# A hybrid decoder layer: the down-projection as seven half-size block products in a phase of its own

## The chip, the cores and the metric

One core of one Trainium2 chip. The metric is the device time of one execution in microseconds (us), as the median of several runs. The kernel is written in Python and fully unrolled. TensorE (PE) multiplies, VectorE (DVE), ScalarE (ACT) and GpSimd (POOL) do elementwise work, and SyncE (SP) issues the DMA transfers. At its end the text is scheduled for a simulated timeline (line 984, `schedule_with_timeline_sim=True`): the order of instructions on each engine comes from there, not from the text.

## The reference

S = 2048 tokens, D = 1024 channels, DFF = 4096, float32:

```
x = x + mix @ w_out                        # mix: gated sum of two attention branches
h2 = rmsnorm(x, ln2_g)
x = x + square(relu(h2 @ w_up)) @ w_down   # w_up: 1024 x 4096, w_down: 4096 x 1024
```

All that stands before (the first norm, the combined input projection, both attentions and the gates) is not touched by the change.

## The kernel before, in words

**Precision.** Each operand of a product is split into a high and a low part of the type float32r: ACT casts the source to the high part (line 91), and DVE or POOL subtracts it from the source for the low part (line 92). `mm3` (lines 94 to 98) makes a product from three matmuls: high x high, low x high, high x low. A matmul takes 128 x 128 stationary and 128 x 512 moving elements, and is preceded by its weight load (PEld).

**Out-projection** (lines 772 to 801). For each of 16 blocks of 128 tokens, `load_mix` loads the mixed activations and x, and splits the former. 2 x 8 x 3 matmuls go to two PSUM banks, DVE adds them to x (line 795), and x is stored to `x2_dram` (line 796). `norm2_pre` forms the RMS scale and the scaled block `hn` (lines 753 to 757). `norm2_post`, one block later, transposes it on PE (line 765), scales it by the norm's gain (line 768) and stores it to `h2_dram` in two transfers of 256 KB whose runs are 512 bytes (line 770).

**MLP** (lines 814 to 966). It goes over two halves of 1024 tokens. The up-projection of a half is made in 16 chunks of 256 columns (f), each a 2 x 2 block matrix product by seven products of half-size blocks instead of eight. A11, A12, A21 and A22 are blocks of w_up, B11 to B22 blocks of the token half (B: which half of D, which 512 tokens). S1 to S4 are sums of the A's and T1 to T4 of the B's. `token_operands` (lines 829 to 856) loads a half from `h2_dram` in four slabs, forms T1 to T4 and splits the seven operands, at the start of each half. `up_operands` (lines 858 to 889) does so for the weights of one chunk, with the sums (line 869) and the low parts on POOL. `up_products` (lines 901 to 939) issues the seven products, 7 x 12 matmuls, into four banks, and combines, squares (lines 913 and 927) and splits the results into `us`, which stay on chip. `down_operands` (lines 891 to 899) loads and splits 2 x 128 rows of w_down, in each half anew. Then 8 blocks x 2 column halves x 2 x 3 = 96 matmuls (line 961) form the chunk's part of the down-projection, and DVE adds each bank to x2 (line 962). At the last chunk the sums are stored to `out` (line 964).

**Buffers.** Most loads pass three shared buffers of 4 KB a partition (`raw`, line 81). PSUM has eight banks (`bank`, line 84). SP's queue issues all the transfers.

Of the kernel before, what the change touches and what calls it, by code (L numbers as in the profile page):

```python
# [20 lines left out]
F32 = mybir.dt.float32  # L21
F32R = mybir.dt.float32r
# [3 lines left out]
ALU = mybir.AluOpType  # L26
# [33 lines left out]
def hybrid_layer(tc, x, positions, ln1_g, w_in, q_norm_a, k_norm_a, q_norm_b, k_norm_b, sinks,  # L60
# [687 lines left out]
    x2_dram = dram.tile([S, D], F32, name="x2_dram")  # L748
    h2_dram = dram.tile([P, KD, S], F32, name="h2_dram")
    x2, hn = {}, {}  # L750
    mpool = pools["A"]

    def norm2_pre(i):
        xt = x2[i]
        rs = rms_scale(xt, tmp(f"junky{i}", BF16, (P, D)), mpool, i, "y")
        hn[i] = B4(f"hn{i}", F32)
        nc.vector.tensor_scalar(hn[i], xt, rs, None, op0=ALU.mult)

    def norm2_post(i):
        xt = hn.pop(i)  # L760
        for half in range(2):
            pt = bank(f"h2ps{i}_{half}")
            for j in range(4):
                k = 4 * half + j
                nc.tensor.transpose(pt[:, j * P:(j + 1) * P], xt[:, k * P:(k + 1) * P], ident)
            ks = slice(4 * half, 4 * half + 4)
            t2 = tmp(f"h2t_{i}_{half}").rearrange("p (j t) -> p j t", j=4)
            nc.vector.tensor_tensor(t2, pt.rearrange("p (j t) -> p j t", j=4),
                                    g2T[:, ks].unsqueeze(2).broadcast_to([P, 4, P]), op=ALU.mult)
            nc.sync.dma_start(h2_dram[:, ks, i * P:(i + 1) * P], t2)  # L770

    def load_mix(i):
        r = raw(f"rmix{i}")
        nc.sync.dma_start(r.rearrange("p (k t) -> p k t", k=KD), mix_dram[:, :, i * P:(i + 1) * P])
        mx = B4(f"mh{i}"), B4(f"ml{i}")
        split(mx[0], mx[1], r)
        x2[i] = B4(f"x2_{i}", F32)
        nc.sync.dma_start(x2[i], x[i * P:(i + 1) * P, :])
        return mx

    wo = []
# [4 lines left out]
    mx = load_mix(0)  # L786
    for i in range(NB):
        nxt = load_mix(i + 1) if i + 1 < NB else None
# [8 lines left out]
        if i > 0:  # L797
            norm2_post(i - 1)
        norm2_pre(i)
        mx = nxt  # L800
    norm2_post(NB - 1)
    for pool in (pools["B"], pools["A"], pools["w"]):
        pool.release()
# [7 lines left out]

    MF = FC // P
    NF = DFF // FC
    SP = [tc.alloc_tile_pool(name="mS", bufs=1, reuse_waits="tile"),
          tc.alloc_tile_pool(name="mD", bufs=1, reuse_waits="tile"),
          tc.alloc_tile_pool(name="mF", bufs=1, reuse_waits="tile"),
          tc.alloc_tile_pool(name="mT", bufs=1, side=RIGHT, reuse_waits="tile"),
          tc.alloc_tile_pool(name="mX", bufs=1, side=RIGHT, reuse_waits="tile")]  # L820
    poolS, poolD, poolF, poolT, poolX = SP
    up_src = w_up.rearrange("(h k p) n -> h p k n", p=P, h=2)
    B_NAMES = ("B11", "T1", "T2", "B21", "T3", "T4", "B22")
    A_NAMES = ("A11", "S1", "S2", "A12", "S3", "A22", "S4")

    def Ft(name):
        return poolF.tile([P, 512], F32, tag="f", bufs=5, name=name)

    def token_operands(hf):

        ops = {n: [poolT.tile([P, 4, 512], F32R, tag="t", bufs=14, name=f"{n}{e}{hf}") for e in "hl"]
               for n in B_NAMES}
        ts = slice(1024 * hf, 1024 * hf + 1024)
        for k in range(4):
            r1, r2 = raw(f"rh1_{hf}_{k}"), raw(f"rh2_{hf}_{k}")
            nc.sync.dma_start(r1, h2_dram[:, k, ts])
            nc.sync.dma_start(r2, h2_dram[:, k + 4, ts])
            b11, b12, b21, b22 = r1[:, 0:512], r1[:, 512:1024], r2[:, 0:512], r2[:, 512:1024]

            def put(n, src, eng):  # L840
                split(ops[n][0][:, k, :], ops[n][1][:, k, :], src, eng)

            put("B11", b11, nc.vector)
            t1, t2 = Ft(f"t1_{hf}_{k}"), Ft(f"t2_{hf}_{k}")
            nc.gpsimd.tensor_tensor(t1, b12, b11, op=ALU.subtract)
            put("T1", t1, nc.vector)
            nc.vector.tensor_tensor(t2, b22, t1, op=ALU.subtract)
            put("T2", t2, nc.vector)
            put("B21", b21, nc.gpsimd)
# [138 lines left out]
```

## Time and profile before

| | |
|---|---|
| median of 3 runs | 2913.75 us (2912.76 to 2917.43) |
| the profiled execution | 2914.77 us; its span, first to last instruction, 2912.7 us |
| busy share of the span | PE 97%, weight loads 81%, DVE 55%, POOL 45%, ACT 37% |
| mean granted PE clock | 0.983 of full |
| DMA traffic | 227 MB, 78 GB/s |

The profile is of one execution. Busy is the time in which an engine ran instructions; the weight loads overlap the matmuls, and matmuls overlap one another in the records, so the pace of PE is read from the number of them in a stretch. The granted clock is the share of PE's 2.4 GHz that the chip let it have.

### The profile page before, as it was taken

What the parts mean: (1) busy time and instruction counts of PE and PEld (TensorE: products, weight loads), DVE (VectorE), ACT (ScalarE), POOL (GpSimd) and SP (SyncE); (2) the same over time, 40 slices, a digit from 0 to 9 for tenths busy, and PEclk for the clock granted to TensorE, in tenths of its full rate; (3) what the DMA queues carried; (4) which work ended last, traced back from release to release, by engine and by line L of the source; (5) the groups of instructions that cost most, each with busy time, mean ns of one, the idle gap of its engine ahead of it and who ended that gap; (6) DMA issues with size and microseconds to landing.
All of it is one profiled execution on the core that took longest, in us unless ns stands there. A gap on an engine that the chain in (4) does not pass through costs nothing.

```text
span 2912.7 us, 37930 instructions
## 1 busy us (share of the span) xinstructions
PE 2827.6 (97%) x14281; PEld 2358.1 (81%) x14281; DVE 1598.6 (55%) x2987; ACT 1069.4 (37%) x2203; POOL 1314.8 (45%) x1148
## 2 busy tenths in 40 slices
PE   7999999999989999999996999999998999999999
PEld 6888888887867888888884888888886788888887
DVE  8777675669984114112336555455557654555455
ACT  5566565667884113112113222222223322222221
POOL 5556666676652111111006545544455654445542
PEclk9999999999999999999996999999999999999999
DMA  5321010011145125224554111111115211111111
GB/s 165 93 73 50 12 55 12 14 56 45 56 123 160 58 66 172 67 67 131 180 174 170 60 46 58 52 57 39 56 58 182 79 59 51 46 49 59 51 58 65
DMA packets 210152, 227.42 MB, mean 78 GB/s; under 512 B 13344, under 2 KB 174128, under 8 KB 209968
## 3 DMA queue, kind: packets, MB, share of 16 engines
q1 hardware_dynamic: 209968, 225.00, 24.6%
q8 instruction: 112, 1.84, 0.3%
q14 instruction: 72, 0.59, 0.1%
HBM read 170.23 MB, written 54.72 MB: 77 GB/s over the span
## 4 chain that ended last, share of the span: by engine, by line
PE 90%; DVE 5%; DMA 2%; POOL 1%; issue 1%; ACT 1%; SPq 0%; POOLq 0%; DVEq 0%; ACTq 0%
PE pd L96 9%; PE pd L97 9%; PE pd L98 9%; PE pg L96 4%; PE pg L98 4%; PE pg L97 4%; PE psA L96 4%; PE psA L97 3%; PE psA L98 3%; PE pb L96 3%; PE pb L97 3%; PE pb L98 3%; PE sp L416 2%; PE pt L461 2%; PE po L97 2%; PE po L96 2%
## 5 line engine op out<-in xcount | busy, mean ns | idle before, releaser
L962 DVE TENSOR_TENSOR x2m<-x2m,pd 128x512 f32<-128x512 f32 x512 | 328.6, 682 | 135.7 <-PE pd L98 135.7
L96 PE MATMUL pd<-wdh,uh 128*128 128x512 f32 x1024 | 398.7, 389 | 0.9 <-ACT uh L91 0.7
L97 PE MATMUL pd<-wdl,uh 128*128 128x512 f32 x1024 | 398.4, 389 | 0.0
L92 POOL TENSOR_TENSOR wdl<-rwd,wdh 128x1024 fp32r<-128x1024 f32 x64 | 152.4, 2405 | 468.1 <-ACT wdh L91 468.1
L98 PE MATMUL pd<-wdh,ul 128*128 128x512 f32 x1024 | 362.1, 389 | 0.5 <-DVE ul L92 0.5
L96 PEld LDWEIGHTS pd<-wdh,uh 128*128 128x128 f32 x1024 | 192.2, 188 | 42.0 <-ACT uh L91 1.7
L98 PEld LDWEIGHTS pd<-wdh,ul 128*128 128x128 f32 x1024 | 192.2, 188 | 40.8 <-DVE ul L92 0.9
L97 PEld LDWEIGHTS pd<-wdl,uh 128*128 128x128 f32 x1024 | 192.2, 188 | 39.9
L91 ACT CAST wdh<-rwd 128x1024 fp32r<-128x1024 f32 x64 | 64.3, 1052 | 408.7 <-PE pd L97 405.0
L96 PE MATMUL psA<-wah,hsh 128*128 128x512 f32 x512 | 209.2, 409 | 3.3 <-DVE mx L420 1.5
L97 PE MATMUL psA<-wal,hsh 128*128 128x512 f32 x512 | 203.0, 396 | 5.7 <-DVE wal L92 5.7
L98 PE MATMUL psA<-wah,hsl 128*128 128x512 f32 x512 | 202.3, 395 | 1.2 <-DVE hsl L92 1.2
L652 DVE TENSOR_TENSOR sig<-sig,pb 128x512 f32<-128x512 f32 x64 | 43.7, 685 | 190.3 <-PE pb L98 169.8
L923 DVE TENSOR_TENSOR fu<-fp,pb 128x512 f32<-128x512 f32 x32 | 22.0, 687 | 227.5 <-PE pb L98 227.5
L312 DVE TENSOR_REDUCE hss<-sq 128x8 f32<-128x512 f32 x64 | 43.8, 685 | 186.3 <-ACT sq L311 186.2
L98 PE MATMUL psB<-wah,hsl 128*128 128x256 f32 x512 | 145.3, 284 | 0.0
L97 PE MATMUL psB<-wal,hsh 128*128 128x256 f32 x512 | 145.1, 283 | 0.0
L96 PE MATMUL psB<-wah,hsh 128*128 128x256 f32 x512 | 143.9, 281 | 0.0
L318 POOL TENSOR_TENSOR hrs<-hss,mhalf 128x8 f32<-128x8 f32 (+1 forms) x64 | 137.1, 2142 | 5.3
L92 POOL TENSOR_TENSOR hsl<-hT,hsh 128x512 fp32r<-128x512 f32 x80 | 118.3, 1479 | 46.0 <-ACT hsh L91 34.5
L91 ACT CAST hsh<-hT 128x512 fp32r<-128x512 f32 x128 | 109.9, 859 | 49.5 <-PE psB L97 44.5
L92 POOL TENSOR_TENSOR wg_1l<-rg,wg_1h 128x1024 fp32r<-128x1024 f32 x16 | 42.3, 2645 | 163.8 <-ACT wg_1h L91 113.8
(520 smaller groups left out, 7572.5 us busy)
## 6 DMA issues: line engine op xcount, KB each, us to landing
rwu<-in_w_up_dram SPq DMA_DIRECT2D x64, 512.0 KB, 3.6
rwd<-in_w_down_dram SPq DMA_DIRECT2D x64, 512.0 KB, 3.9
x<-in_x_dram SPq DMA_DIRECT2D x32, 512.0 KB, 4.1
rg<-in_w_in_dram SPq DMA_DIRECT2D x32, 512.0 KB, 4.1
rw<-in_w_in_dram SPq DMA_DIRECT2D x28, 384.0 KB, 3.3
hT_dram<-hT SPq DMA_DIRECT2D x16, 512.0 KB, 3.9
mix_dram<-sig SPq DMA_DIRECT2D x32, 256.0 KB, 2.0
rmix<-mix_dram SPq DMA_DIRECT2D x16, 512.0 KB, 4.0
```

Source lines behind the costliest of these rows:

```text
L91: nc.scalar.copy(hi, src)
L92: (eng or nc.vector).tensor_tensor(lo, src, hi, op=ALU.subtract)
L96: nc.tensor.matmul(out, lhs[0], rhs[0], start=first, stop=False, skip_group_check=more)
L97: nc.tensor.matmul(out, lhs[0], rhs[1], start=False, stop=False, skip_group_check=more)
L98: nc.tensor.matmul(out, lhs[1], rhs[0], start=False, stop=last, skip_group_check=more)
L312: nc.vector.tensor_reduce(ss[:, 0:8], sq, axis=AX, op=ALU.add)
L318: nc.gpsimd.tensor_tensor(rs[:, 0:nh], ss[:, 0:nh], mhalf[:, 0:nh], op=ALU.pow)
L416: nc.tensor.matmul(sp[:, e * 256:e * 256 + nk], ring[:, own, q_, :], ring[:, slots, k_, :], start=(i == 0), stop=(i == 1))
L461: nc.tensor.transpose(pt[:, h * P:(h + 1) * P], p[4 * q4 + h][:, kb * P:(kb + 1) * P], ident)
L652: nc.vector.tensor_tensor(gate[m, c, a], gate[m, c, a], pb, op=ALU.mult)
L923: nc.vector.tensor_tensor(u2, p1, bb, op=ALU.add)
L962: nc.vector.tensor_tensor(x2[i][:, ns], x2[i][:, ns], pd, op=ALU.add)
```

## The change

The order of blocks in the out-projection alternates between the two 512-token quarters of a half. With a pair of them, `norm2_post` forms T1 to T4 on POOL, block by block, and stores the seven token operands, unsplit, to `b_dram` (seven stores of 256 KB a pair, runs of 512 bytes). `token_operand` loads and splits one of them. Four of the first half's are split during the out-projection, three after it; those of the second half in chunks 12, 13 and 15 of the first.

The MLP becomes two phases. In the up phase, 2 x 16 chunks run with no down-products between them. `up_products` uses three banks; its results are combined and squared on ACT and DVE into seven operands u of the second product, and these are stored, unsplit, to `u_ops_dram` (1.84 MB a chunk, runs of 512 bytes). Two of `up_operands`' four sums go to DVE, and there are 12 instead of 10 buffers for its operands.

In the down phase the down-projection too is made by seven half-size products instead of eight. It runs over 8 pairs of chunks (F) and 4 groups of tokens (g). For each group and product, `u_operand` loads 256 KB, ACT and POOL split it into one of nine buffers, PE does 12 matmuls, and DVE adds the bank to the accumulators, which now hold all the tokens. The seven operands of w_down for the next F are formed and split in the text between groups 1 and 2 (`next_down_operands`), so w_down is loaded and split once and not once a half. The core of the diff:

```diff
+    PRODUCTS = (("A11", "B11"), ("S1", "T1"), ("S2", "T2"), ("S4", "B22"), ("S3", "T3"), ("A12", "B21"),
+                ("A22", "T4"))
+    BANKS = (0, 1, 0, 1, 0, 2, 0)
+    pools["B"].release()
+    pools["A"].release()
+    poolT1 = tc.alloc_tile_pool(name="mT1", bufs=1, side=RIGHT, reuse_waits="tile")
...
     def norm2_post(i):
+        hf, c, j = i // 8, i // 4 % 2, i % 4
...
-            nc.sync.dma_start(h2_dram[:, ks, i * P:(i + 1) * P], t2)
+        if c == 0:
+            keep("B11", hb[0, 0])
+            keep("B21", hb[1, 0])
+            return
+        keep("B22", hb[1, 1])
+        def summed(n, a, b):
+            t = poolO.tile([P, 4, P], F32, tag="hsum", bufs=3, name=f"hsum{n}_{i}")
+            nc.gpsimd.tensor_tensor(t, a, b, op=ALU.subtract)
+            keep(n, t)
+            return t
+        t1 = summed("T1", hb[0, 1], hb[0, 0])
...
+    def token_operand(hf, o):
+        n = B_NAMES[o]
+        pool = poolT1 if (o < 4 if hf == 0 else 2 <= o < 6) else pools["T2"]
...
+        for q in range(2):
+            r = raw(f"rb{hf}_{n}_{q}")
+            ks = slice(2 * q, 2 * q + 2)
+            rv = r.rearrange("p (k t) -> p k t", k=2)
+            nc.sync.dma_start(rv, b_dram[hf][n][:, ks, :])
+            split(t[0][:, ks, :], t[1][:, ks, :], rv, nc.gpsimd if q else nc.vector)
...
+        put("S4", summed("4", a12, s2, ALU.subtract, nc.vector))
+        put("S3", summed("3", a11, a21, ALU.subtract, nc.vector))
...
+    order = [8 * hf + 4 * c + j for hf in range(2) for j in range(4) for c in range(2)]
...
+        if 10 <= n < 14:
+            token_operand(0, n - 10)
+    A_next = up_operands(0, 0)
+    norm2_post(order[-1])
+    poolO.release()
+    pools["w"].release()
...
+    def up_products(hf, f, A, B, then):
+        u = poolU.tile([P, 7, 512], F32, tag="u", bufs=2, name=f"u_{hf}_{f}")
...
+            elif i == 4:
+                nc.vector.tensor_tensor(a22, a22, p, op=ALU.add)
+                relu2(a22)
+                nc.vector.tensor_tensor(u[:, 1, :], a21, a22, op=ALU.add)
+            elif i == 5:
+                nc.vector.tensor_tensor(a11, a11, p, op=ALU.add)
+                relu2(a11)
+                nc.vector.tensor_tensor(u[:, 2, :], u[:, 1, :], a11, op=ALU.subtract)
+                nc.vector.tensor_tensor(u[:, 4, :], a11, a21, op=ALU.subtract)
+            else:
+                relu2(a12, p)
+                nc.vector.tensor_tensor(u[:, 3, :], a12, u[:, 2, :], op=ALU.subtract)
+            then(i)
+        nc.sync.dma_start(u_ops_dram[hf][f // 2][:, :, :, f % 2, :], u.rearrange("p o (j t) -> p o j t", j=4))
...
+            def then(i):
+                if hf == 0 and last and i < 5:
+                    token_operand(1, i + 2)
+            up_products(hf, f, A, Bops[hf], then)
+            if f + 1 < NF or hf == 0:
+                A_next = up_operands(hf + last, 0 if last else f + 1)
+            if hf == 0 and f in (NF - 4, NF - 3):
+                token_operand(1, f - (NF - 4))
+            if hf == 1 and f == NF - 5:
+                first_down_operands()
...
+    for p in range(8):
+        a = poolT1.tile([P, 2, D], F32, tag="t", bufs=8, name=f"acc{p}")
+        for c in range(2):
+            i = 8 * (p // 4) + 4 * c + p % 4
+            nc.sync.dma_start(a[:, c, :], x2_dram[i * P:(i + 1) * P, :])
+        acc.append(a)
...
+    def u_operand(F, g, o):
+        hf, j = g // 2, 2 * (g % 2)
+        r = raw(f"ru{F}_{g}_{o}")[:, 0:512]
+        nc.sync.dma_start(r.rearrange("p (j f t) -> p j f t", j=2, f=2), u_ops_dram[hf][F][:, o, j:j + 2, :, :])
+        t = poolV.tile([P, 2, 512], F32R, tag="v", bufs=9, name=f"uo{F}_{g}_{o}")
+        split(t[:, 0, :], t[:, 1, :], r, nc.gpsimd)
...
+    for F in range(NFF):
+        for g in range(4):
+            ps = [[bank(f"pd{F}_{g}_{q}_{b}") for b in range(3)] for q in range(2)]
+            for i in range(7):
+                U = u_operand(F, g, i)
+                if F == 0 and g == 0 and i == 0:
+                    next_down_operands(0, B_NAMES[4:7])
+                w = Wops[F, B_NAMES[i]]
+                first = i in (0, 1, 5)
+                for q in range(2):
+                    p = ps[q][BANKS[i]]
+                    for f in range(2):
+                        mm3(p, [U[:, e, q, f, :] for e in range(2)], [w[:, e, f, :] for e in range(2)],
+                            f == 0 and first, f == 1, not first)
...
+                    nc.vector.tensor_tensor(t, t, p, op=ALU.add)
...
+            if g == 1 and F + 1 < NFF:
+                next_down_operands(F + 1, B_NAMES)
```

## Rows read from the trace of the kernel before

**Rows 1.** The page's first part: each engine's busy time, its share, its instructions.

```profile
PE 2827.6 (97%) x14281; PEld 2358.1 (81%) x14281; DVE 1598.6 (55%) x2987; ACT 1069.4 (37%) x2203; POOL 1314.8 (45%) x1148
```

**Rows 2.** Stretches: from:to, length, busy (count) PE, PEld, DVE, ACT, POOL; clock, DMA share, GB/s.

```profile
1410.00:1420.00 10.00, 10.00 (x50) 8.38 (x49) 4.46 (x6) 2.09 (x3) 0.79 (x2) 1.00 0.58 186
...
1560.00:1570.00 10.00, 1.62 (x3) 0.50 (x2) 4.47 (x4) 2.25 (x5) 3.57 (x3) 0.50 0.94 385
...
1540.00:1600.00 60.00, 32.18 (x93) 20.80 (x92) 40.58 (x35) 23.90 (x41) 43.41 (x31) 0.60 0.54 184
2220.00:2280.00 60.00, 49.53 (x188) 36.66 (x188) 50.16 (x58) 24.32 (x41) 40.34 (x25) 0.86 0.69 245
...
2000.00:2200.00 200.00, 200.00 (x884) 165.62 (x883) 108.02 (x145) 47.46 (x72) 93.24 (x63) 1.00 0.16 50
```

**Rows 3.** Waits of PE: who for whom, us in total, times, the longest.

```profile
PE pa L96 <- ACT B11h L91: 14.8, 4, 6.6
...
PE pb L97 <- DVE T2l L92: 7.0, 4, 1.9
PE h2ps L765 <- DVE hn L757: 6.6, 1, 6.6
```

**Rows 4.** Timeline: the last addition of the span of 2912.7 us.

```profile
2908.90 0.69 DVE L962 TENSOR_TENSOR x2m<-x2m,pd 128x512 f32<-128x512 f32 x1 [0.67 <-PE pd L98]
```

**Rows 5.** Groups of instructions: the down-projection's matmuls (one of three lines), and their addition.

```profile
L962 DVE TENSOR_TENSOR x2m<-x2m,pd 128x512 f32<-128x512 f32 x512 | 328.6, 682 | 135.7 <-PE pd L98 135.7
L96 PE MATMUL pd<-wdh,uh 128*128 128x512 f32 x1024 | 398.7, 389 | 0.9 <-ACT uh L91 0.7
```

**Rows 6.** Timeline of SP's queue in the out-projection: two store issues.

```profile
1402.12 1.09 SPq L770 DMA_DIRECT2D h_dram<-h2t  x2
```

**Rows 7.** DMA issues of the kernel: KB each, median us to landing.

```profile
rwu<-in_w_up_dram SPq DMA_DIRECT2D x64, 512.0 KB, 3.6
...
h_dram<-h2t SPq DMA_DIRECT2D x32, 256.0 KB, 3.2
...
x2m<-x_dram SPq DMA_DIRECT2D x16, 512.0 KB, 7.4
out_dram<-x2m SPq DMA_DIRECT2D x32, 256.0 KB, 2.2
```

**Rows 8.** Groups in the steady MLP, 1700 to 2200: busy us, mean ns.

```profile
L913 DVE SCALAR_TENSOR_TENSOR fu<-fu 128x512 f32<-128x512 f32 x24 | 40.3, 1678 | 0.4
...
L930 DVE TENSOR_TENSOR fu<-fp,pb 128x512 f32<-128x512 f32 x12 | 8.2, 686 | 18.2 <-PE pb L98 18.2
...
L92 POOL TENSOR_TENSOR wdl<-rwd,wdh 128x1024 fp32r<-128x1024 f32 x25 | 59.5, 2403 | 208.1 <-ACT wdh L91 208.1
L869 POOL TENSOR_TENSOR s<-rwu 128x512 f32<-128x512 f32 x12 | 20.9, 1739 | 0.0
...
L92 POOL TENSOR_TENSOR A11l<-rwu,A11h 128x512 fp32r<-128x512 f32 x12 | 15.5, 1292 | 0.0
...
L91 ACT CAST wdh<-rwd 128x1024 fp32r<-128x1024 f32 x26 | 26.1, 1052 | 179.5 <-PE pd L97 179.5
...
L91 ACT CAST A11h<-rwu 128x512 fp32r<-128x512 f32 x12 | 7.5, 622 | 25.7 <-PE pb L97 25.7
...
L926 ACT ACTIVATE fc<-pa 128x512 f32<-128x512 f32 x12 | 7.1, 593 | 0.0
```

**Rows 9.** Groups in the out-projection, 1350 to 1540.

```profile
L92 DVE TENSOR_TENSOR ml<-rmix,mh 128x1024 fp32r<-128x1024 f32 x16 | 19.9, 1245 | 1.7 <-ACT mh L91 1.7
```

**Rows 10.** DMA queues in the out-projection, 1400 to 1500: packets, MB, share of 16 engines.

```profile
DMA packets 20304, 18.00 MB, mean 180 GB/s; under 512 B 688, under 2 KB 18096, under 8 KB 20300
...
q1 hardware_dynamic: 20300, 17.94, 56.2%
```

**Rows 11.** Timeline of PE in a steady chunk: first matmuls of T4's and T3's products.

```profile
1759.46 0.39 PE L96 MATMUL pd<-T4h,A22h 128*128 128x512 f32 x1
...
1761.96 0.39 PE L96 MATMUL pb<-T3h,S3h 128*128 128x512 f32 x1
```

More of the change, by code (lines that the diff above doesn't have):

```diff
@@ L796, in hybrid_layer @@
         nc.sync.dma_start(x2_dram[i * P:(i + 1) * P, :], x2[i])
-        if i > 0:
-            norm2_post(i - 1)
+        if n > 0:
+            norm2_post(order[n - 1])
         norm2_pre(i)
+        if 10 <= n < 14:
+            token_operand(0, n - 10)
         mx = nxt
[L801 to L824, printed above, removed]
-    def Ft(name):
[L827 to L849, printed above, removed]
-            t3, t4 = Ft(f"t3_{hf}_{k}"), Ft(f"t4_{hf}_{k}")
-            nc.gpsimd.tensor_tensor(t3, b22, b12, op=ALU.subtract)
-            put("T3", t3, nc.vector)
-            nc.vector.tensor_tensor(t4, b21, t2, op=ALU.subtract)
-            put("T4", t4, nc.vector)
-            put("B22", b22, nc.gpsimd)
-        return ops
@@ new lines, in hybrid_layer, with down_operands @@
+    Wops = {}
+    def down_operands(F, ns, fs, quarter, temp):
+        ts = {}
+        for n in B_NAMES:
+            for f in fs:
+                b = [[quarter(f, m, n_) for n_ in range(2)] for m in range(2)]
+                if n[0] == "B":
+                    src = b[int(n[1]) - 1][int(n[2]) - 1]
+                else:
+                    x_, y_ = {"T1": (b[0][1], b[0][0]), "T2": (b[1][1], ts.get(f)), "T3": (b[1][1], b[0][1]),
+                              "T4": (b[1][0], ts.get(f))}[n]
+                    if n in ("T3", "T4") and n not in ns:
+                        continue
+                    src = ts[f] if n in ("T2", "T4") else temp(n, f)
+                    nc.vector.tensor_tensor(src, x_, y_, op=ALU.subtract)
+                    if n == "T1":
+                        ts[f] = src
+                if n in ns:
+                    if (F, n) not in Wops:
+                        Wops[F, n] = pools["T2"].tile([P, 2, 2, 512], F32R, tag="t", bufs=10, name=f"w{n}_{F}")
+                    t = Wops[F, n]
+                    split(t[:, 0, f, :], t[:, 1, f, :], src, nc.gpsimd)
@@ new lines, in down_rows, with first_down_operands, next_down_operands @@
+    def down_rows(F, f, m):
+        t0 = (2 * F + f) * FC + m * P
+        return slice(t0, t0 + P)
+    def first_down_operands():
+        for f in range(2):
+            r = []
+            for m in range(2):
+                r.append(raw(f"rwd0_{f}_{m}"))
+                nc.sync.dma_start(r[m], w_down[down_rows(0, f, m), :])
+            down_operands(0, B_NAMES[0:4], [f], lambda f, m, n: r[m][:, n * 512:(n + 1) * 512],
+                          lambda n, f: Ft(f"w{n}s0_{f}"))
+    def next_down_operands(F, ns):
+        b = {}
+        for f in range(2):
+            for m in range(2):
+                for n in range(2):
+                    b[f, m, n] = poolS.tile([P, 512], F32, tag="S", bufs=12, name=f"rwd{F}_{f}_{m}_{n}")
+                    nc.sync.dma_start(b[f, m, n], w_down[down_rows(F, f, m), n * 512:(n + 1) * 512])
+        down_operands(F, ns, range(2), lambda f, m, n: b[f, m, n],
+                      lambda n, f: poolS.tile([P, 512], F32, tag="S" if n == "T1" else "s",
+                                              bufs=12 if n == "T1" else 2, name=f"w{n}s{F}_{f}"))
@@ L965, in hybrid_layer @@
-    for pool in (poolX, poolT, edge, poolF, poolD, poolS, dram, psp, rawp, const):
+            last = f == NF - 1
+            def then(i):
[8 more added lines that the diff above has]
+                first_down_operands()
```

202 lines of the change are left out of this document (98 added, 104 removed).

## The prediction

> **What bounds the kernel now.** I read the busy line first, then the stretches, then what TensorE (PE) waited for, then the durations of what stands beside it. PE is busy 97% of the span and no other engine passes 55% [rows 1]; the weight loads of the busy line overlap the matmuls. In the MLP's steady stretch PE never pauses at full clock: 884 matmuls start in 200 us, 0.2262 us each [rows 2]. There POOL is busy 47%, DVE 54%, ACT 24%, the DMA engines 16%. So time there is the number of matmuls times 0.2262. Two stretches are different: the hand-over from the out-projection to the MLP, and the one between the two token halves. In 1540 to 1600 PE runs 93 matmuls where 60 us hold 265, so 60 - 93 x 0.2262 = 39 us are lost, and in the middle its granted clock is 0.50 of full, the lower of its two levels, 1.2 GHz, after PE had been idle; in 2220 to 2280 it runs 188, and 17 us are lost [rows 2]. Both are waits for the last transposes and for the token operands, B11 and T2 above all [rows 3]. The tail is short: the last add starts 3.8 us before the end [rows 4].
>
> **Matmuls removed.** The down-projection is 3 x 1024 matmuls of 512 columns [rows 5]. After the change it is 8 pairs of chunks x 4 groups x 7 products x 12 = 2688; the up-projection keeps 32 x 7 x 12 = 2688. Gone are 384 x 0.2262 = **86.9 us**, all on the path, as PE is what ends every steady stretch.
>
> **Hand-over to the MLP.** The seven token sums are now formed block by block in the out-projection, and four of the seven operands are split there too. Per pair of blocks (96 matmuls and the transposes, over 22 us) this adds four POOL sums, 4 x 1.3 to 1.7 us, and three more 256 KB stores; four operands add 8 casts, 4 DVE and 4 POOL subtractions over four blocks. A 10 us slice there has DVE busy 4.5, ACT 2.1, POOL 0.8 us, DMA 58% [rows 2]: all of it is covered by PE. If that cover were gone, the POOL sums would cost 8 x 4 x 1.5 = 48 us. SP's issues are 0.5 us each [rows 6], so its queue is not late. When the out-projection ends, PE has 4 products, 48 x 0.2262 = 10.9 us, ready. The other three operands wait for the space of the out-projection's tiles and pass three raw buffers, of which the first f-chunk's weights hold one until the first product is over. Each takes a load (3.6 us [rows 7]), two casts, and a POOL subtraction of 2.4 us [rows 8]; the third is done about 18 us in, and is needed at 16.3; the next chunk's weights come behind it in the same buffers. I take 5 us left of the 39; bounds 0 and 39.
>
> **Hand-over between the halves.** Two operands are split in chunks 12 and 13, five in the last chunk, each when its predecessor's product has freed the slot. The window for these is 12 products, 32.6 us. Ten token loads and two weight loads through three raw buffers, at an estimated 7.5 us each (load 3.6, cast 1.05, subtraction 1.2 on DVE [rows 9] or 2.4 on POOL, and gaps), need 12 x 7.5 / 3 = 30 us: just enough. The casts that wait for a freed slot stand in ACT's queue before the same chunk's squares; those only delay u's store, which has a second buffer of 19 us. I take 5 us of the 17; bounds 0 and 17.
>
> **Steady up-projection.** A chunk is now 84 x 0.2262 = 19.0 us with no down-products between. POOL: seven subtractions of 1.29 and two sums of 1.29 to 1.74, 12.0 us. ACT: 7 x 0.62 + 11 x 0.59 = 10.8 us. DVE: three adds from PSUM at 0.69, six with both inputs in SBUF at 0.69 to 1.68, 6 to 12 us [rows 8]. A weight operand has 12 buffers, so it may be made five products (13.6 us) ahead. The new u store is 1.84 MB in runs of 512 bytes. The out-projection's traffic, half of it in such runs, moves 180 GB/s at 56% [rows 10], 320 GB/s if never idle: 5.7 us. The lower end is 4.8 us at the 385 GB/s of a busy slice [rows 2], the upper is seven times the 3.2 us of a 256 KB store, 22 us [rows 7]; I take 5.7, since those 3.2 us contain a latency that one large store pays once. With the weights' loads that is about 9 us of 19, and u has two buffers: no cost. At 22 us the DMA engines would need 25 of 19 us, 32 x 6 = 190 us; I give that 0.02, counted with D below.
>
> **Steady down-projection.** A pair of chunks is 336 matmuls, 76.0 us. POOL: 28 operand splits and 14 weight splits, 42 x 1.3 = 55 us; DVE: 56 adds at 0.68 and 8 sums, 44 us; ACT 26 us. Loads of 256 KB must come every 2.71 us through three raw buffers: a store of that size takes 2.2 us to land [rows 7], so (2.2 + 0.62 + 1.3) / 3 = 1.4 us each. No cost. PSUM holds 6 of 8 banks and each add has one product, 2.7 us, before its bank is written again.
>
> **Start of the down phase.** The accumulators are 16 loads of 512 KB, 8.4 MB, 22 us at 385 GB/s [rows 2]; eight such loads in a row show 7.4 us to land where one of the weights takes 3.6 [rows 7]. The u loads queue behind them, and several u buffers lie where the last u tile waits for its store. The accumulators may start four products early, so between 0 and 20 us may be lost; I take 6. Where the first down weights take the raw buffers, and in the out-projection, I add 3, between 0 and 10. That w_down is now loaded and split once instead of twice (64 casts of 1.05 and 64 subtractions of 2.4 us become 112 and 112 of half the size) lies beside PE before and after, and gains nothing.
>
> **Sum.** The profiled execution took 2914.8 us, 1.0 above the median. 2914.8 - 86.9 - 39 - 17 + 5 + 5 + 6 + 3 = 2790.9, less 1 is **2790**.
>
> **Rivals.**
> *A. The hand-overs stay as long as they are.* The operands would be late for another reason, the raw buffers and the DMA queue. For: three raw buffers for everything, 30 of 32.6 us needed. Against: four operands are ready before the out-projection ends. 2790 + 34 + 12 = 2836. Chance 0.10.
> *B. DVE and POOL hold each other up.* Beside a busy POOL, DVE's instruction with both inputs in SBUF takes 1.68 us, the PSUM add 0.69; POOL's sum takes 1.74 where others take 1.29 [rows 8]. In the up phase the add that frees bank 0 may stand behind two such sums: 2 x 1.68 + 0.69 = 4.05 us against 2.71, 1.3 us lost in each of 32 chunks, 42 us: 2832. For: six such instructions a chunk are new in kind. Against: POOL and they together are 12.0 + 6 x 0.69 = 16.2 of 19.0 us, so mostly they find room. Chance 0.06. The Trainium skill, SBUF — State Buffer, Who interferes with whom, says that a DVE instruction with two SBUF inputs contends with a GpSimd instruction that reads SBUF, and speaks against moving work to exactly this form; the two durations agree with it, and at worst its time is the one given here.
> *C. The u operands' buffers.* If a 256 KB load takes the 7.4 us of queued ones, the loop is (7.4 + 0.62 + 1.3) / 3 = 3.11 us against 2.71, 0.4 x 224 operands = 90 us: 2880. From 7.9 us on all is lost. Against: the DMA engines would be 35% busy there. Chance 0.06, a third of it ending within 0.2%.
> *D. Slower: the next weights stand ahead of the u operands.* In the text, the 14 weight splits of the next pair come between groups 1 and 2. Were the engines' queues in that order, POOL would run 14 x 1.3 = 18 us, and the first u operand 2 us, with PE dry, 7 times: 140 us, 2930 (before any clock loss). It decides from 17.5 us a time. Against: nothing keeps the text's order; PE starts T4's product before T3's [rows 11], which the text has the other way round, so the order follows readiness, and nine operand buffers allow 24 us of lead. Chance 0.08.
>
> **How the numbers follow.** Forecast 0.70, A 0.10, B 0.06, C 0.06, D 0.08. About 0.2%, 6 us, is what a measurement here can tell from no change. Faster: 0.70 + 0.10 + 0.06 + 0.04 = 0.90; same 0.02; slower 0.08. The low end is the sum with no new cost, 2771; the high end takes in A and B and the upper bounds of the down phase's start, 2850. C and D stay outside.
>
> **What would show it.** Right: 384 fewer matmuls; PE dense at full clock in both phases; less than 12 us lost at the two hand-overs together; no PE wait longer than 10 us where the down phase begins. Wrong: PE waiting for POOL's u operands after every second group (D), waits of 1 to 2 us on DVE in each chunk (B), loads of u over 6 us (C), a granted clock of 0.50 where the MLP begins (A).

## The result, and the profile after

The changed kernel takes 2842.49 us (median of four runs, 2841.38 to 2846.34) where before took 2914.09 beside it: a ratio of 0.9755 [0.9738, 0.9772]. That is 72 us less. The forecast was 2790 in a range of 2771 to 2850, so the sign and the range held, and the gain was 52 us smaller than forecast. The profiled execution took 2842.3 us, its span 2840.4.

The busy line of after, which answers to [rows 1]:

```profile
PE 2736.9 (96%) x13897; PEld 2284.1 (80%) x13897; DVE 1510.6 (53%) x2821; ACT 1287.2 (45%) x2607; POOL 1569.5 (55%) x1370
```

PE issues 14281 - 13897 = 384 matmuls fewer, the number of the prediction. Next the stretches of after that answer to [rows 2], of PE alone: from:to, length, busy (count), granted clock, DMA share, GB/s. The first three are the hand-over from the out-projection to the MLP, the one between the token halves, and the start of the down phase; the last two are the steady phases.

```profile
1520.00:1600.00 80.00, 66.58 (x280) 0.91 0.64 202
1860.00:1900.00 40.00, 24.88 (x96) 0.83 0.78 247
2180.00:2260.00 80.00, 55.19 (x225) 0.85 0.81 279
1620.00:1840.00 220.00, 220.00 (x972) 1.00 0.52 159
2300.00:2800.00 500.00, 500.00 (x2207) 1.00 0.44 126
```

Both steady phases are as forecast: PE never stops, 220 / 972 = 0.2263 us a matmul at full clock. What is missing is in the first three rows. The loss of a stretch is its length less its matmuls at 0.2262 us. At the half boundary it is 40 - 96 x 0.2262 = 18.3 us, at the down start 80 - 225 x 0.2262 = 29.1 us. At the hand-over to the MLP 32 of the 280 are transposes. A block of 48 matmuls and 8 transposes takes 11.5 us where the out-projection runs full (194 instructions in 40 us), which leaves 0.09 us for a transpose, and 80 - 248 x 0.2262 - 32 x 0.09 = 21 us are lost. Together 68 us. Before lost 17 us between the halves, and at its hand-over 41 rather than the 39 of the prediction, since 16 of the 93 instructions counted there are transposes (60 - 77 x 0.2262 - 16 x 0.09). So 86.9 - (68 - 58) = 77 us of gain are left, and 72.3 lie between the spans; part of the rest is a wait of 1.9 us at the first product of the out-projection (1356.12), where before has none of that size.

PE's waits of after (who for whom, us in total, times, the longest), which answer to [rows 3]:

```profile
PE pd L96 <- ACT uo L91: 23.7, 1, 23.7
PE pa L96 <- ACT A11h L91: 11.4, 1, 11.4
...
PE h2ps L795 <- DVE hn L780: 8.5, 3, 4.6
```

Each of the three stretches has its wait: for the first operand of the down phase (uo), for the first up weight of the second half (A11h), and for the norm of the last token tiles (hn). The DMA issues, which answer to [rows 7] (KB each, median us to landing):

```profile
u_dram<-u SPq DMA_DIRECT2D x32, 1792.0 KB, 7.6
ru<-u_dram SPq DMA_DIRECT2D x224, 256.0 KB, 2.7
rwu<-in_w_up_dram SPq DMA_DIRECT2D x64, 512.0 KB, 3.8
```

The u loads land in 2.7 us, and the u store takes 7.6 where 5.7 was taken, well inside a chunk of 19 us.

**The down start, read.** The granted clock fell with the idle time (from:to, length, then PE, PEld, DVE, ACT, POOL, clock, DMA share, GB/s):

```profile
2200.00:2220.00 20.00, 0.00 (x0) 0.00 (x0) 4.05 (x7) 2.27 (x4) 4.97 (x4) 0.60 1.04 405
2220.00:2240.00 20.00, 17.21 (x61) 12.98 (x62) 12.92 (x15) 8.70 (x15) 18.74 (x13) 0.80 0.89 301
```

No compute engine is busy for more than a quarter of the first row, and the DMA engines are full at 405 GB/s. In the second row the 61 matmuls take 17.21 us, 3.4 more than at full clock; the first twelve of them start within 4.86 us (2222.35 to 2227.21), 2.4 more than at full clock. The timeline of ACT in after says what PE waited for:

```profile
2205.23 0.62 ACT L91 CAST wT<-wT3s 128x512 fp32r<-128x512 f32 x1 [5.28 <-DVE wT3s L974]
...
2220.56 0.62 ACT L91 CAST wT<-wT3s 128x512 fp32r<-128x512 f32 x1 [9.11 <-DVE wT3s L974]
2221.16 0.62 ACT L91 CAST wT<-wT1s 128x512 fp32r<-128x512 f32 x1
2221.69 1.66 ACT L91 CAST uo<-ru 128x512 fp32r<-128x512 f32 x3
```

and that of SP's queue:

```profile
2185.22 0.33 SPq L1046 DMA_DIRECT2D ru<-u_dram  x1
...
2186.95 6.14 SPq L1036 DMA_DIRECT2D acc<-x_dram  x4
...
2203.94 5.97 SPq L1036 DMA_DIRECT2D acc<-x_dram  x6
2210.22 0.33 SPq L1003 DMA_DIRECT2D rwd<-in_w_down_dram  x1
```

The first three u operands were loaded early (the third load is issued at 2185), but their casts stand on ACT behind six casts of weights that only the fifth product and those after it need. The last of those weights (the load at 2210.22) is issued behind sixteen accumulator loads. My theory: ACT's order and the full DMA together make the 23.7 us. The rival: u's cast waits for its slot, which the last u store must leave.

### The profile page after: what moved, and what is told of

Same layout as the page of the kernel before. It is cut to its first block, busy times and chain, and to the rows that moved or that the text cites. A ratio compares the mean times of both kernels' runs of the same rounds, so it can differ in the third digit from the quotient of the medians.

```text
span 2840.4 us, 38633 instructions
## 1 busy us (share of the span) xinstructions
PE 2736.9 (96%) x13897; PEld 2284.1 (80%) x13897; DVE 1510.6 (53%) x2821; ACT 1287.2 (45%) x2607; POOL 1569.5 (55%) x1370
## 4 chain that ended last, share of the span: by engine, by line
PE 85%; DVE 5%; DMA 4%; POOL 3%; issue 2%; ACT 1%; SPq 0%; POOLq 0%; ACTq 0%; DVEq 0%
PE pd L96 7%; PE pd L98 7%; PE pd L97 7%; PE pg L98 4%; PE pg L96 4%; PE pg L97 4%; PE pa L96 4%; PE pa L98 4%; PE pa L97 4%; PE psA L96 4%; PE psA L98 3%; PE psA L97 3%; PE pb L98 3%; PE pb L96 3%; PE pb L97 3%; PE pt L461 2%
## 5 line engine op out<-in xcount | busy, mean ns | idle before, releaser
L1071 DVE TENSOR_TENSOR acc<-acc,pd 128x512 f32<-128x512 f32 x448 | 298.6, 684 | 212.9 <-PE pd L98 212.9
L92 POOL TENSOR_TENSOR uo<-ru,uo 128x512 fp32r<-128x512 f32 x224 | 305.1, 1371 | 159.4 <-ACT uo L91 155.6
L91 ACT CAST uo<-ru 128x512 fp32r<-128x512 f32 x224 | 138.2, 621 | 343.1 <-PE pd L98 219.3
L97 PE MATMUL pd<-wT,uo 128*128 128x512 f32 x512 | 199.7, 390 | 0.0
L96 PE MATMUL pd<-wT,uo 128*128 128x512 f32 x512 | 198.3, 391 | 0.3 <-ACT wT L91 0.3
L98 PE MATMUL pd<-wT,uo 128*128 128x512 f32 x512 | 196.7, 389 | 0.0
L96 PE MATMUL pd<-wB,uo 128*128 128x512 f32 x384 | 150.4, 392 | 24.0 <-ACT uo L91 23.7
L97 PE MATMUL pd<-wB,uo 128*128 128x512 f32 x384 | 150.1, 391 | 0.0
L98 PE MATMUL pd<-wB,uo 128*128 128x512 f32 x384 | 149.1, 391 | 0.0
L98 PEld LDWEIGHTS psA<-wah,hsl 128*128 128x128 f32 x512 | 96.9, 189 | 21.3 <-DVE hsl L92 1.4
```

Source lines behind the costliest of these rows:

```text
L91: nc.scalar.copy(hi, src)
L92: (eng or nc.vector).tensor_tensor(lo, src, hi, op=ALU.subtract)
L96: nc.tensor.matmul(out, lhs[0], rhs[0], start=first, stop=False, skip_group_check=more)
L97: nc.tensor.matmul(out, lhs[0], rhs[1], start=False, stop=False, skip_group_check=more)
L98: nc.tensor.matmul(out, lhs[1], rhs[0], start=False, stop=last, skip_group_check=more)
L1071: nc.vector.tensor_tensor(t, t, p, op=ALU.add)
```

## The experiments

The runs, in three groups, each group beside before on one chip (after in a fourth, by itself); "against after" is the difference of the ratios times 2914 us. Each ratio is known to 4 or 5 us, so a difference against after of less than about 6 us is not clear of the noise.

| run | median us | ratio to before, 95% | against after, us |
|---|---|---|---|
| after | 2842.49 | 0.9755 [0.9738, 0.9772] | |
| e1b_acc_later | 2832.88 | 0.9719 [0.9705, 0.9732] | -10.5 |
| e8_act_order | 2851.95 | 0.9784 [0.9770, 0.9797] | +8.5 |
| e9b_both | 2837.79 | 0.9735 [0.9722, 0.9749] | -5.8 |
| e10_three_first | 2830.82 | 0.9716 [0.9702, 0.9729] | -11.4 |
| e4_up_first | 2844.08 | 0.9757 [0.9744, 0.9770] | +0.6 |
| e5_raw4 | 2851.13 | 0.9783 [0.9770, 0.9797] | +8.2 |
| e5b_raw4_up_first | 2846.34 | 0.9768 [0.9755, 0.9781] | +3.8 |
| e12_boundary | 2840.33 | 0.9748 [0.9732, 0.9764] | -2.0 |
| e6b_norm_first | 2840.04 | 0.9746 [0.9732, 0.9759] | -2.6 |
| e11_all_three | 2827.93 | 0.9699 [0.9686, 0.9712] | -16.3 |
| e13_sums_on_dve | 2823.54 | 0.9687 [0.9674, 0.9701] | -19.8 |
| e14_spare_u_buffer | 2818.83 | 0.9671 [0.9658, 0.9685] | -24.5 |

What an edit does at its own place is seen better in the one trace of each run, between the starts of the same two matmuls, since a window of fixed time moves over the work when an earlier stage gets shorter. Three such stretches are used below. The MLP stretch goes from the first product of the out-projection to 170 matmuls into the MLP and takes 250.9 us in after (247.1 to 250.9 in the seven runs that leave it alone, after among them). The boundary stretch goes from 170 matmuls before the second half to 170 into it: 95.8 us (95.8 to 97.2 in six such runs). The down stretch goes from 170 matmuls before the first down product to 170 behind it: 106.5 us (106.2 to 107.4 in four such runs).

### The start of the down phase

**e1b_acc_later.**

```diff
+    load_acc(0)
+    load_acc(1)
...
                 U = u_operand(F, g, i)
+                if F == 0 and g < 3 and i == 4:
+                    with tc.issue_after(getattr(ru_dma[0], "ins", ru_dma[0])):
+                        load_acc(2 * g + 2)
+                        load_acc(2 * g + 3)
```

> Twelve of the sixteen accumulator loads (6.3 of 8.4 MB) are queued behind the operand loads of the row-block pair before, so they leave the start of the down phase; the order of the casts on ACT stays. Theory (the phase starts late because ACT has to cast the second half of the first down weights before the first u operand, and those weights share a full DMA with the accumulators): the weights land some 10 to 15 us sooner, PE's wait for uo falls from 23.7 us to 9 to 14 us, the run gets 10 to 15 us shorter than after. Rival 1 (only the order of the casts counts, the loads were not late): within 3 us of after. Rival 2 (the first u operand waits for the slot that the last u store must leave): that store also goes out sooner here, so a gain of about 10 us fits too; the next run tells it apart.

The run is 10.5 us shorter, and the wait is halved:

```profile
PE pd L96 <- ACT uo L91: 11.0, 1, 11.0
```

The last two weight casts ahead of uo come at 2212.02 and 2213.69, and uo at 2214.21, in a kernel whose phase began 5 us later. The down stretch takes 95.4 us, 11 less than in after. So the accumulator loads are worth 10 us there, as the theory had it. The edit takes twelve of them out of the full DMA and out of SP's queue ahead of the weights, and does not separate the two.

**e8_act_order.**

```diff
+        casts.append(nc.scalar.copy(t[:, 0, :], r))
...
+    Us = [u_operand(0, 0, o) for o in range(4)]
+    with tc.issue_after(getattr(casts[-1], "ins", casts[-1])):
+        next_down_operands(0, B_NAMES[4:7])
...
-                if F == 0 and g == 0 and i == 0:
-                    next_down_operands(0, B_NAMES[4:7])
```

> The accumulator loads stay as in after; only the order on ACT is changed: the casts of the first four u operands stand ahead of the casts of the T3, B21 and T4 weights. Theory (the late first operand stands behind those casts on ACT): PE's wait for uo shrinks from 23.7 to under 8 us, the first four products (48 matmuls, 10.9 us) run in the gap, and PE then waits some 10 to 13 us for the T3 weight instead; the run is 8 to 11 us shorter. Rival (the operand itself is late: its slot or its data): uo is not cast earlier, PE's wait stays over 20 us, and the run is within 3 us of after.

The run is 8.5 us longer, so both expectations of the time fall; its down stretch takes 114.5 us, 8 more than in after. The timeline of ACT in this run:

```profile
2199.66 1.64 ACT L1048 CAST uo<-ru 128x512 fp32r<-128x512 f32 x3
2230.22 0.62 ACT L1048 CAST uo<-ru 128x512 fp32r<-128x512 f32 x1 [28.92 <-DMA ru<-u_dram]
2230.75 1.14 ACT L91 CAST wT<-wT3s 128x512 fp32r<-128x512 f32 x2
```

The first three casts run at 2199.66, 22 us earlier than in after, right behind the last up chunk. That refutes the rival for these three: no slot and no data was missing. But I had put four casts ahead, and the fourth operand's load stands in SP's queue behind the accumulators and the weight loads of the first and the second pair, so the weights now wait 28.92 us behind it. And before that PE stops for something else, on DVE:

```profile
2210.09 0.69 DVE L974 TENSOR_TENSOR wT1s<-rwd,rwd 128x512 f32<-128x512 f32 x1 [4.17 <-issue]
2218.88 0.69 DVE L974 TENSOR_TENSOR wT1s<-rwd,wT1s 128x512 f32<-128x512 f32 x1 [8.10 <-DMA rwd<-in_w_down_dram]
...
2220.69 2.48 DVE L1074 TENSOR_TENSOR acc<-acc,pd 128x512 f32<-128x512 f32 x4
```

The sums of the same weights stand in DVE's queue ahead of the adds that empty PE's banks. PE waits for them:

```profile
PE pd L96 <- DVE acc L1074: 15.4, 1, 15.4
```

So the late loads hold PE through DVE as they did through ACT, and this order of ACT's queue gained nothing while the loads were late. Three casts ahead, with the loads left as they are, were not tried.

**e9b_both** joins the two edits, four casts ahead and the accumulators later.

> Both edits: accumulators later and the u casts first. Theory: the loss of the down start (28.7 us in 2180 to 2260 of after) falls to 6 to 12 us and the run is 17 to 23 us shorter than after, more than either edit alone. Rival (the two edits remove the same wait): no shorter than the better of the two within 3 us.

Between the two: 5.8 us shorter than after, 4.7 longer than e1b_acc_later, with a down stretch of 100.3 us. PE's waits here are 7.1 us for uo in three pieces, 4.7 for its low part and 3.8 for the adds. The forecast of 17 to 23 us falls.

**e10_three_first** changes e9b_both in two places: three casts stand ahead instead of four, and the second pair's weight loads are queued behind the u loads.

```diff
-    Us = [u_operand(0, 0, o) for o in range(4)]
+    Us = [u_operand(0, 0, o) for o in range(3)]
...
-                next_down_operands(F + 1, B_NAMES)
+                with tc.issue_after(getattr(ru_dma[0], "ins", ru_dma[0])):
+                    next_down_operands(F + 1, B_NAMES)
```

> Accumulators later as in e1b_acc_later, only three u casts (the loads that stand early in SP's queue) ahead of the casts of the first weights, and the loads of the second chunk pair's weights queued behind the u loads of the first two groups. Theory (three heads of queues: ACT's order, SP's order, the full DMA): no cast stands behind a late load now; PE starts the phase within 4 us, may wait up to 8 us for the T3 weight or for the fourth operand, the loss in 2180 to 2260 of after (28.7 us) falls to 8 to 13 us, and the run is 14 to 20 us shorter than after, 5 to 10 us shorter than e1b_acc_later. Rival (what starts sooner only waits longer for the second half of the weights): PE's wait moves whole to the T3 weight, and the run is within 3 us of e1b_acc_later.

PE never stops for longer than 3.9 us now (columns as above):

```profile
2200.00:2220.00 20.00, 14.83 (x52) 11.70 (x53) 13.30 (x15) 7.24 (x14) 16.07 (x12) 0.83 0.88 309
2220.00:2240.00 20.00, 20.00 (x90) 16.54 (x89) 12.45 (x17) 6.49 (x11) 12.14 (x10) 1.00 0.88 303
```

From 2160 to 2300 it runs 566 matmuls, against 489 in after and 538 in e1b_acc_later: 17.4 and 6.3 us, what the theory expected; the down stretch takes 88.3 us. But by the ratios the run is only 0.9 us shorter than e1b_acc_later, where 5 to 10 were expected, because from 2300 on it gives 2208 - 2179 = 29 matmuls back, 6.6 us. In that stretch DVE waits for the loads that this edit moved back (2290 to 2420), and the clock falls (PE alone):

```profile
DVE wT1s L974 <- DMA rwd<-in_w_down_dram: 6.1, 2, 5.2
```

```profile
2300.00:2340.00 40.00, 37.06 (x151) 0.91 0.49 150
```

So the loads and the queues of SP, ACT and DVE together explain the loss at the start, and the second edit of e10 moved part of it to the next weights. The time is the rival's, within 3 us of e1b_acc_later, but not for its reason: PE's wait did not move to the T3 weight (1.1 us on wT in all). What the third cast and the moved weight loads are worth each was not tried.

### The boundary of the halves

**e4_up_first** writes the second half's first up weights ahead of the five token operands.

```diff
+            if hf == 0 and last:
+                A_next = up_operands(1, 0)
             up_products(hf, f, A, Bops[hf], then)
```

> At the boundary of the halves the loads and splits of the second half's first up weights are written ahead of the five token operands, so they get the raw buffers first. Theory (A11 is late by its place in the queue): the 11.4 us wait of PE for A11h goes, the loss in 1860 to 1900 falls from 18 to 4 to 8 us, and the run is 9 to 14 us shorter than after. Rival (three raw buffers and ACT are the limit whatever comes first): PE waits as long for a token operand (T3, B21 or T4 of the second half) instead, and the run is within 3 us of after.

The time does not move. The boundary stretch takes 93.6 us, 2 less than in after: the wait for A11h is gone, and PE runs 370 matmuls from 1840 to 1940 instead of 360, but in the waits of this run the token operands are late in its place (1840 to 1930):

```profile
PE pa L96 <- ACT T4h L91: 3.0, 1, 3.0
PE pa L96 <- ACT a L936: 2.1, 1, 2.1
PE pb L97 <- POOL B22l L92: 1.9, 1, 1.9
```

That is the rival: the order only picks which operand is late.

**e5_raw4** and **e5b_raw4_up_first** add a fourth raw buffer, the second with the order of e4.

```diff
-    rawp = tc.alloc_tile_pool(name="rawp", bufs=3)
+    rawp = tc.alloc_tile_pool(name="rawp", bufs=4)
...
-            t2 = hb[half, c] = poolO.tile([P, 4, P], F32, tag="hb", bufs=6, name=f"hb{i}_{half}")
+            t2 = hb[half, c] = poolO.tile([P, 4, P], F32, tag="hb", bufs=5, name=f"hb{i}_{half}")
...
-        t = poolV.tile([P, 2, 512], F32R, tag="v", bufs=9, name=f"uo{F}_{g}_{o}")
+        t = poolV.tile([P, 2, 512], F32R, tag="v", bufs=8, name=f"uo{F}_{g}_{o}")
```

> A fourth raw buffer (paid for by one hb buffer of six and one u-operand slot of nine). Theory (the hand-over of the halves and the one to the MLP are paced by load, cast and low part through three raw buffers): the loss in 1860 to 1920 falls from 18 to 8 to 13 us and that in 1520 to 1600 from 19 to 12 to 16; the run is 7 to 14 us shorter than after. Rival 1 (the order of SP's queue sets it): A11h waits as before, within 3 us. Rival 2 (the fifth hb buffer is missed): waits of h2ps or hb in the out-projection, slower by up to 10.

> Four raw buffers and the second half's first up weights ahead of the token operands. Theory (raw buffers pace the boundary and the order only says which operand is late): the boundary's loss falls to 5 to 9 us, and the run is 3 to 6 us shorter than e5_raw4. Rival (order counts for nothing): the same as e5_raw4 within 2 us.

At the boundary both do what the theory says. The 100 us from 1840 to 1940 of e5b_raw4_up_first, of PE alone (after: 84.88 busy, x360, clock 0.93; e5_raw4: x384):

```profile
1840.00:1940.00 100.00, 95.44 (x411) 0.98 0.64 202
```

51 matmuls more than after, 11.5 us, and the loss of the stretch is 100 - 411 x 0.2262 = 7 us. The boundary stretch takes 84.4 us in e5b_raw4_up_first and 90.5 in e5_raw4, and between the two runs lie 4.4 us, as expected. Yet e5_raw4 is 8.2 us longer than after, and e5b_raw4_up_first 3.8, which is inside the noise. In e5_raw4 the norm of the last token tiles is later, 15.1 us of waits instead of 8.5:

```profile
PE h2ps L795 <- DVE hn L780: 15.1, 3, 8.3
```

and PE falls behind in a stage that has nothing to do with the MLP, 919 instructions in after and here, in e5b_raw4_up_first:

```profile
800.00:1000.00 200.00, 182.75 (x878) 0.96 0.38 113
```

The raw buffers serve every stage; there and in the out-projection the edit costs more than it brings at the boundary. The first product of the out-projection starts at 1368.9 and 1367.5 in these two, and between 1354.4 and 1360.1 in the eleven others. Neither hb nor v buffers are in use before it, so the missing ones are not the reason; how a further raw buffer slows the stages before is open.

**e12_boundary** therefore gives the fourth buffer to the boundary alone (every fourth load of the last chunk), with the order of e4.

```diff
+        if spare[0]: spare[0] += 1
+        return poolF.tile([P, D], F32, tag="fr", bufs=1, name=name) if spare[0] and spare[0] % 4 == 0 else rawp.tile([P, D], F32, tag="raw", name=name)
...
             last = f == NF - 1
+            spare[0] = int(hf == 0 and last)
```

> After with the second half's first up weights ahead of the token operands and a fourth raw buffer there alone (every fourth load at the boundary, in space that the up phase leaves free), so that no other stage changes. Theory (the boundary is paced by three raw buffers, and order only picks the late operand): PE's waits of the boundary fall as in e5b_raw4_up_first, the 100 us from 1840 to 1940 hold 400 to 411 matmuls instead of 360, and the run is 9 to 12 us shorter than after. Rival (four buffers helped through the stages before): up to 375 matmuls there as in e4_up_first, within 3 us of after.

My theory fails here: PE alone, from 1840 to 1940,

```profile
1840.00:1940.00 100.00, 90.41 (x368) 0.95 0.62 187
```

which is the 370 of e4_up_first and the time of after within 2 us (the four runs spread over 13 us, 2834.99 to 2847.96). The boundary stretch takes 94.0 us. Both the count and the time are what the rival expected. A fourth buffer for the last chunk's loads alone is not what helped e5b_raw4_up_first. The two traces differ in SP's order: here the store of the last u tile is issued at 1886.33 and the last token load (T4) behind it, cast at 1895.38; there both T4 loads go out at 1899.75, ahead of the store at 1905.95, and PE has no wait for T4h. Behind a u store a load is late: this T4 load lands after 8.4 us, where the eight token loads before it take 3.4 to 4.7; in e5b_raw4_up_first the load behind a store is one of B22 (8.3 us), and PE does not wait for it. After shows the same. SP's queue there, and the landing of the first load behind the store at 1867.32 (KB, us):

```profile
1867.32 0.53 SPq L953 DMA_DIRECT2D u_dram<-u  x1
1870.74 3.12 SPq L840 DMA_DIRECT2D rb_B<-b_dram_B  x2
1874.67 7.10 SPq L840 DMA_DIRECT2D rb_T<-b_dram_T  x2
1883.89 1.47 SPq L852 DMA_DIRECT2D rwu<-in_w_up_dram  x2
```

```profile
rb_B<-b_dram_B SPq DMA_DIRECT2D x1, 512.0 KB, 8.3
```

That this order is the reason is read from the queues and was not tried. The wait for T4h in e12_boundary is 3.2 us, a part only of the 10 us between the two stretches.

### The hand-over to the MLP

In after the norm of a token tile is late for a reason that has nothing to do with it. Its timeline, ACT, POOL and DVE in turn:

```profile
1520.40 0.62 ACT L91 CAST A11h<-rwu 128x512 fp32r<-128x512 f32 x1 [4.68 <-DMA rwu<-in_w_up_dram]
```

```profile
1521.10 1.28 POOL L92 TENSOR_TENSOR A11l<-rwu,A11h 128x512 fp32r<-128x512 f32 x1 [2.36 <-ACT A11h L91]
1522.34 1.27 POOL L808 TENSOR_TENSOR hsumT<-hb,hsumT 128x512 f32<-128x512 f32 x1
1523.57 1.26 POOL L808 TENSOR_TENSOR hsumT<-hb,hb 128x512 f32<-128x512 f32 x1
1524.79 0.57 POOL L127 TENSOR_TENSOR rsxy<-ssy,mhalf 128x1 f32<-128x1 f32 x1
```

```profile
1525.39 1.74 DVE L780 TENSOR_SCALAR hn<-x,rsxy 128x1024 f32<-128x1024 f32 x1 [7.39 <-POOL rsxy L127]
```

The low part of the first up weight stands on POOL ahead of the norm's power, and waits for a weight that has not landed; two of the new token sums follow it. **e6b_norm_first** changes only that order.

```diff
-    A_next = up_operands(0, 0)
+    with tc.issue_after(norms[-2][0]), tc.issue_after(norms[-2][1]):
+        A_next = up_operands(0, 0)
```

> Only issue order on ACT and POOL at the end of the out-projection: the splits and sums of the first up weights stand behind the square and the power of the last token tile but one. Theory (the norm of a token tile waits on POOL and ACT behind A11, whose weight was not loaded yet): PE's wait h2ps <- hn falls from 8.5 to 3 to 5 us, and the loss in 1520 to 1600 from 19 to 12 to 15; the run is 4 to 8 us shorter than after. Rival (the up weights are then the late ones, by as much): h2ps waits less, but PE waits for A11, S1 or S2 at the start of the MLP, and the run is within 3 us of after.

```profile
PE h2ps L795 <- DVE hn L780: 6.8, 2, 4.9
```

The wait that the chain above ends in, 4.6 us at 1527 in after and 2.5 to 4.6 in the seven runs that leave this place alone, is gone here and in e11_all_three, which has the same edit. The wait for the last block stays and grows from 3.0 to 4.9 us: its norm begins with the end of the out-projection, and its transposes stand on PE ahead of the first product of the MLP (1557.77 in after). PE runs 488 instructions from 1500 to 1620 instead of 460, 6.3 us; but the runs that leave this place alone have 459 to 477, and e11_all_three has 475. The MLP stretch takes 245.4 us, 247.0 in e11_all_three. So the edit is worth some 2 to 5 us at its place. The run is 2.6 us shorter, with intervals that overlap: between theory and rival. From 1620 to 1840 the two kernels are equal, but PE runs 354 matmuls at the half boundary instead of 360 and 486 at the down start instead of 489.

### Together

**e11_all_three** joins e10, e6b and e12.

> The edits of e10_three_first, e6b_norm_first and e12_boundary together. Theory (three separate hand-overs, so the gains add): 11.7 + 2.5 + 9 to 12 us, so 20 to 27 us shorter than after, 2816 to 2822 us, some 93 to 98 below before. Rival (one clock or queue ties them): under 17 us.

16.3 us by the ratios, under the rival's bound. But the measured parts are 11.4 + 2.6 + 2.0 = 16.0, so the time agrees with gains that add, as far as parts of 2 us inside the noise can say, and the forecast was too high by what e12 did not bring.

**e13_sums_on_dve** adds one edit to e11_all_three, and **e14_spare_u_buffer** one more.

```diff
-            nc.gpsimd.tensor_tensor(t, a, b, op=ALU.subtract)
+            nc.vector.tensor_tensor(t, a, b, op=ALU.subtract)
             keep(n, t)
```

> As e11_all_three, with the four token sums of each pair on DVE instead of POOL. Theory (the square root of the last token tiles waits on POOL behind these sums): PE's wait h2ps <- hn falls from about 7 to 2 to 4 us, and the run is 2 to 5 us shorter than e11_all_three. Rival (DVE's order takes the place of POOL's): the same within 2 us, or slower.

3.5 us shorter, as the theory had it in size, but the wait for hn goes only from 6.1 to 5.0 us: the small waits before are gone, that for the last block stays. The MLP stretch takes 243.2 us against 247.0 in e11_all_three, and 244.6 in the next run, which has the same edit; e6b_norm_first, which has not, takes 245.4. A gain of 1 to 4 us lies at the place of the edit, no more than that stretch scatters, and the boundary stretch, which the edit does not touch, is 2.2 us shorter too. The theory is not shown.

```diff
-        r = raw(f"ru{F}_{g}_{o}")[:, 0:512]
+        r = poolV.tile([P, 512], F32, tag="rv", bufs=1, name=f"ru{F}_{g}_{o}") if F == 0 and (7 * g + o) % 4 == 3 else raw(f"ru{F}_{g}_{o}")[:, 0:512]
```

> As e13_sums_on_dve, with a fourth buffer for the loads of the u operands in the first chunk pair of the down phase. Theory (what is left at the start of the down phase are u loads through three buffers): the stretch of 2160 to 2300 (in its own time, after the last up product) loses 3 to 6 us less and the run is 3 to 5 us shorter than e13_sums_on_dve. Rival (the full DMA, or the weights, set it): within 2 us.

4.7 us shorter than e13, as the theory had it. From the last up product to the end of the first 336 down products it takes 87.4 us, where e13 takes 90.2 and e11, with three buffers too, 88.5: 2.8 us against e13, just under the 3 to 6 expected. The next 336 products, whose loads do not use the buffer, take 76.2 us instead of 80.4. Whether the buffer does that, or the order of the queues that comes out with it, stays open. At 2818.83 us this version beats both kernels: ratio 0.9671 [0.9658, 0.9685], 24.5 us below after.

## Why the prediction was right in sign and 52 us short

**Matmuls removed: right.** 384 fewer, 86.9 us, and both steady phases are at the pace of [rows 2].

**Steady phases: right.** No wait of PE from 1620 to 1840 or after 2300, so rivals B, C and D fall. Two of DVE's sums with both inputs in SBUF, from 1620 to 1840 (busy us, mean ns):

```profile
L947 DVE TENSOR_TENSOR u<-u 128x512 f32<-128x512 f32 x12 | 20.0, 1666 | 0.4
...
L948 DVE TENSOR_TENSOR u<-u,a 128x512 f32<-128x512 f32 x12 | 8.3, 692 | 16.9 <-ACT u L925 8.7 <-ACT a L925 8.2
```

The first always meets POOL instructions and takes 1.67 us; the second meets none in eleven of the twelve chunks and takes 0.69, no more than a PSUM add. That is the contention that the Trainium skill states (SBUF — State Buffer, Who interferes with whom), but it never reaches PE. The u loads take 2.7 us, not the 7.4 of C. For D, PE never waits between the groups, so the next weights do not hold up the u operands there.

**Start of the down phase: the largest miss, 29 us for 6, outside its own bound of 20.** The step said that "the u loads queue behind" the accumulators, and that u's slots wait for the store. For the first three operands neither holds: their loads were early, and the casts could run at 2199.66 (e8). For the fourth the first half does (28.92 us in e8). What the step left out is the order on ACT and DVE: weights for the fifth product stood ahead of the operands of the first, and were themselves late through the accumulators. The working that dismissed D held for the groups, and I did not ask the same question of the first group, where the weights are not ready ahead. Taking most accumulator loads away gave 10.5 us; with the order and the next pair's loads put right too (e10), PE ran 17 us more work at the start.

**Hand-over between the halves: 18 us for 5, rival A's size there.** The working had "need 12 x 7.5 / 3 = 30 us: just enough". What failed is the evenness that it took: loads of 3.6 us each, begun all through the window. The first slab of T2 landed at 1847.63 and was cast only at 1857.48, so one of the three buffers stood full for 10 us; and the three loads behind the u store at 1867.32 landed after 8.3, 6.9 and 6.9 us. The first up weights came behind ten token loads in the same buffers; moving them ahead alone (e4) only made a token operand late. Four buffers in every stage with the other order brought the loss to 7 us; a fourth that only the last chunk's loads use did not (e12), so that the number of buffers is the pace, as the step had it, is not shown, and what each of these delays makes of the 18 us is open.

**Hand-over to the MLP: 21 us for 5.** The step looked at the last three token operands. They cost PE 4.4 us in waits (T4h 2.3, B21l 1.5, T3l 0.6). The larger wait, 7.5 us, is for the norm: 4.6 behind the weight split on POOL, and 3.0 for the last block, whose transposes stand ahead of the four products that the step counts as ready. "All of it is covered by PE" held for busy time, not for order: the POOL instruction that waited, through ACT, for a load delayed the three behind it. Changing that order removed the first wait; some 2 to 5 us of it stayed gained at this place, 2.6 by the ratios.

**The sum.** 5 + 5 + 6 + 3 = 19 us were left in the forecast, 68 in the trace; rival A, which kept the old hand-overs, came nearest with 2836. The difference of 49, less the 2 us by which the 39 was read too low, is most of the 51.4 between the unrounded sum, 2790.9, and the profiled 2842.3. That the range held is in part luck: the down start lost 9 us more than its upper bound, and the hand-over to the MLP 18 less than rival A, whose time the range takes in. Of the four signs of being right two came (384 matmuls fewer, dense phases) and two did not: the two hand-overs lost 39 us, not under 12, and PE waited 23.7 us where the down phase begins, not under 10.

## What to carry to other kernels

Where a phase begins, write down for each in-order queue (SP, ACT, DVE, POOL) what stands ahead of the first operand and when that is loaded; a share of busy time says nothing of it. Move the loads that are not needed yet out of the way first, and the order of the casts only then: alone, the reordering with four casts made the kernel slower. Ask what large store stands ahead of a load that is due. A buffer that serves all stages acts in all of them: here a fourth gained 11 us at one hand-over, with an order change, and lost more elsewhere. And compare traces between the same two instructions, with a few runs that leave the place alone beside them.

## What was not expected of the hardware

The store of 1.84 MB in runs of 512 bytes landed in a median of 7.6 us, 241 GB/s, beside other traffic. Loads of 512 KB issued behind it landed after 8.3 us (B21 in after) and 8.4 (T4 in e12), where others at that place take 3.4 to 4.7. A pause of PE costs more than its length: with the 23.7 us the granted clock was 0.60 in the slice of 20 us that lies in the pause and 0.80 in the next, where 61 matmuls took 17.2 us instead of 13.8; with the pause cut to 11.0 us (e1b) the two slices had 0.74 and 0.91, and with none longer than 4 us (e10) 0.83 and 1.00.
